# A pooling and state-space layer on one core: decode states turned together, and staged through DRAM

## The chip, the cores and the metric

The kernel runs on one core of a Trainium2 chip. TensorE multiplies matrices (PE in the profile; PEld is its loading of weights), VectorE is DVE, ScalarE is ACT, GpSimd is POOL, and SyncE (SP) issues DMAs. ACT issues DMAs too. Sixteen DMA engines move the data. The metric is the time of one execution on the device in microseconds, as the median of several runs.

## The reference

One layer is applied to a prompt (1 x 1024 tokens) and to eight decode samples of 8 tokens each. The model width is 1024; the input projection has 8224 columns.

```python
h = rmsnorm(x, norm_g) * (1 + scale[:, None]) + shift[:, None]
u_pool, z_pool, z_ssm, xbc, dt_raw, g_raw = jnp.split(h @ w_in, SPLITS, axis=-1)
p, pool_new = pool_mix(u_pool, pool_buf, pos0, pool_w, pool_scale)   # last 15 input rows kept
p = (p * jax.nn.silu(z_pool)) @ w_pool_out
xbc_c, conv_new = causal_conv(xbc, conv_buf, conv_w, conv_b)         # width 4, last 3 rows kept
y, ssm_new = ssd(xs, dt, A, Bm, Cm, ssm_state)                       # 32 heads of 64 x 128
y = rmsnorm((y + d_skip * xs) * jax.nn.silu(z_ssm), ssm_norm_g)
m = gates[..., :D_MODEL] * p + gates[..., D_MODEL:] * (y @ w_ssm_out)
x = x + gate[:, None] * (m @ w_o)
```

The samples bring states from earlier steps: `state_pool` (8 x 15 x 512), `state_conv` (8 x 3 x 3072) and `state_ssm` (8 x 32 x 64 x 128). The prompt starts from zero. The outputs are y for prompt and samples and the new states of both: the last 15 pooling rows, the last 3 convolution rows and the state matrices. Everything is float32.

## The kernel before

Channels lie on the 128 partitions and tokens along the free axis, 1088 of them: 1024 of the prompt, then 64 of the samples. A product in float32 is made of three passes in fp32r, a faster format, on operands that are split into a high and a low part; the split takes ACT (`whi`) and POOL or DVE (`wlo`).

The program has four stages. The first (`first`) normalizes x, makes the adaLN factors and starts the projection. The second goes through `units`, pairs of 128 columns of `w_in`. Each pair is one Strassen product of seven half products (`product`, lines 609 to 611), and its two column blocks go to a generator that finishes them: `to_dram` for the gates ("light" pairs), `conv_unit`, `u_unit` and `zp_unit` ("heavy" pairs). The steps of a generator that come after its product wait in the list `later` and are taken out one by one between the half products of the next pair (`between`, `step`); what is left is taken at the last. Beside the pairs runs `splits`, which prepares weights of later stages and sends them to DRAM.

The third stage runs the last ten light pairs with `samples_beside`: first the steps of `dt_end`, then for each of four head groups `ssd_samples`, 18 steps apiece, spread evenly. The fourth does the prompt's chunks, the output products and the norms; its loop is not touched.

The order of instructions on an engine in the first stage and the last is written out by hand (`in_line`). In the second and third stage a planner orders them by a simulated time line; `behind(engine)` only says that an instruction comes after the last one on an engine that was written before it. Each queue of DMA issues runs in order, so a DMA that waits holds those behind it. A tile with `bufs=n` has n slots in rotation; a new tile waits until the slot's last user is done.

What the change touches:

- `conv_unit` (line 1031): per block of 128 channels it loads the samples' 24 state rows into `stc`, turns them on PE (1039) and lets ACT copy them (1040). Later it collects the last rows of prompt and samples in `t27` (1049, 1051), turns them (1067), copies them (1069), and ACT issues two stores (1070, 1071). This happens for 24 blocks.
- `u_unit` (757): the same for four blocks with 120 state rows (`stp`, 760, 775, 776), and with turns of the 15 and 64 last rows (805, 806).
- `ssd_samples` (1223): `h0_load` (1239) reads four batches of two heads straight from `state_ssm` into one of four tiles `h0`, in runs of 512 bytes. A step turns four 128 x 128 blocks with a float32 identity (1304), copies them (1306), and `update` (1288) makes the new state in place in `h0` (1294), which ACT's queue stores (1296).
- `turn_r` (117): a turn in fp32r, so far used by the chunk stage alone; its instructions have line 118.
- `dt_end` (1077): loads the raw dt rows into `s0`, a tile of tag `dec`, and turns them (1109).
- `to_conv` (1553): closes the first stage's right-hand memory and opens that of the convolutions, whose big tiles have tag `GA` (seven slots).

Of the kernel before, what the change touches and what calls it, by code (L numbers as in the profile page):

```python
# [8 lines left out]
F32 = mybir.dt.float32  # L9
# [37 lines left out]
def tile_pool_ssd_step(  # L47
# [9 lines left out]
    def nm(s):  # L57
        uid[0] += 1
        return f"{s}_{uid[0]}"
# [36 lines left out]
    def PB():  # L96
        return psB.tile([P, 512], F32, tag="ps", name=nm("ps"))
# [40 lines left out]
    nc.gpsimd.memset(rc[:, 0:1], 1.0)  # L138
    vb = sm.tile([44, P], F32, tag="stc", name="vb", bufs=4)
    store_(vb[0:16, :], b_ada[0, 0:2048].rearrange("(m p) -> m p", p=P))  # L140
# [231 lines left out]
    def late_loads():  # L372
        va = sm.tile([120, P], F32, tag="stc", name="va", bufs=4)
# [7 lines left out]
        dx = sm.tile([16, 2, 64], F32, tag="stc", name="dx", bufs=4)  # L381
# [375 lines left out]
    def u_unit(gi):  # L757
        L = gi + 1
        stp = sm.tile([120, P], F32, tag="stc", name=nm("stp"), bufs=4)
        load(stp, state_pool[0, :, :, gi * P:(gi + 1) * P].rearrange("b t c -> (b t) c"))  # L760
        pwt = sm.tile([P, P], F32, tag="stc", name=nm("pwt"), bufs=4)
        load(pwt, pool_w[0, gi])
# [10 lines left out]
        V.memset(up[:, 0:15], 0.0)  # L773
        ps = PB()
        nc.tensor.transpose(ps[:, :120], stp, ident[:120, :120])
# [34 lines left out]
        store_(new_pool_p[0, 0, :, gi * P:(gi + 1) * P], o15)  # L810
        store_(new_pool_s[0, :, 7:15, gi * P:(gi + 1) * P], o64)
        y = up[:, :T]
# [216 lines left out]


    def conv_unit(mc, dst):
# [7 lines left out]
        nc.tensor.transpose(ps[:, :24], stc, ident[:24, :24])  # L1039
        act(seg[:, :, 0:3], ps[:, :24].rearrange("p (b t) -> p b t", t=3), AF.Copy)  # L1040

# [23 lines left out]
        store_(dst[:, SEQ:], s64.rearrange("p b t -> p (b t)"))  # L1065
        ps = PB()
        nc.tensor.transpose(ps[:27, :P], t27, ident)
# [9 lines left out]
    def dt_end():  # L1077
# [145 lines left out]
    def ssd_samples(g):  # L1223
# [5 lines left out]
        load_E(E2, g)  # L1229
        dec = spt([P, 8, P], "dec", 2)[:NS, :, :NS]  # L1230
        decays(dec, g, NC)
# [4 lines left out]
        def h0_load(j):  # L1236
            hf, q = divmod(j, 4)
            h0 = spt([P, 4, P], "h0", H0B)
            load(h0, state_ssm[0, 4 * hf:4 * hf + 4, 8 * g + 2 * q:8 * g + 2 * q + 2].rearrange("b h p n -> (h p) b n"))
            h0s[j] = h0  # L1240
# [19 lines left out]
        for hf in range(2):  # L1260
# [27 lines left out]
            def update(r):  # L1288
                h0 = h0s.pop(4 * hf + r)
                pu = PB()  # L1290
                mm(pu, xh[:96, r * P:(r + 1) * P], Bb[:96].rearrange("p b n -> p (b n)"), start=True, stop=True)
                for b in range(4):
                    cc_ = 32 * hf + 8 * b + 7
                    V.scalar_tensor_tensor(h0[:, b, :], h0[:, b, :], E2[:, r, cc_:cc_ + 1],
                                           pu[:, b * P:(b + 1) * P], ALU.mult, ALU.add)
                store_(new_ssm_s[0, 4 * hf:4 * hf + 4, 8 * g + 2 * r:8 * g + 2 * r + 2]
                       .rearrange("b h p n -> (h p) b n"), h0)
            for q in range(4):
# [4 lines left out]
                for b in range(4):  # L1303
                    nc.tensor.transpose(pt[:, b * P:(b + 1) * P], h0s[j][:, b, :], ident)
                hts[q] = spt([P, 512], ("hT", "yt", "hU", "hV")[q], 1)
# [247 lines left out]
    def to_conv():  # L1553
        nonlocal right
        right.__exit__(None, None, None)
        right = tc.tile_pool(name="ga", bufs=1, side="right", reuse_waits="tile")
        gas.append(right.__enter__())

    def to_ssd():
# [291 lines left out]
    def m_split(k, mem):  # L1851

        sh = sm.tile([P, P], F32R, tag="stc", name=nm("sh"), bufs=4)
        act(sh[:, 0:NS], acc[k][:, SEQ:], AF.Copy)
# [200 lines left out]
```

## Time and profile before

| | us |
|---|---|
| median of 3 runs | 1273.08 (1272.99 to 1273.53) |
| the profiled execution | 1271.29 |
| its span, first to last instruction | 1269.5 |
| PE busy | 1242.3 (98%) |
| DVE busy | 900.9 (71%) |
| ACT busy | 718.0 (57%) |
| POOL busy | 683.1 (54%) |

The profile page has the busy time of each engine, the costliest groups of instructions, and the DMA queues. Queries to the trace give the busy time by stretch, the waits (an engine and line that waited, who ended it, total us, number and longest), all instructions of one line (minimum, median and longest duration in ns, first and last start), and a timeline. Matmuls are pipelined: the next starts before the last has ended, so durations on PE overlap and start times tell more. Sixteen engines share the DMA packets; they carried 234.90 MB in this execution.

### The profile page before, as it was taken

What the parts mean: (1) busy time and instruction counts of PE and PEld (TensorE: products, weight loads), DVE (VectorE), ACT (ScalarE), POOL (GpSimd) and SP (SyncE); (2) the same over time, 40 slices, a digit from 0 to 9 for tenths busy, and PEclk for the clock granted to TensorE, in tenths of its full rate; (3) what the DMA queues carried; (4) which work ended last, traced back from release to release, by engine and by line L of the source; (5) the groups of instructions that cost most, each with busy time, mean ns of one, the idle gap of its engine ahead of it and who ended that gap; (6) DMA issues with size and microseconds to landing.
All of it is one profiled execution on the core that took longest, in us unless ns stands there. A gap on an engine that the chain in (4) does not pass through costs nothing. (4 is left out here: it accounts for less than half of the span.)

```text
span 1269.5 us, 26341 instructions
## 1 busy us (share of the span) xinstructions
PE 1242.3 (98%) x9771; PEld 1173.9 (92%) x9771; DVE 900.9 (71%) x1584; ACT 718.0 (57%) x1683; POOL 683.1 (54%) x555
## 2 busy tenths in 40 slices
PE   7999999999999999999999999999999999999997
PEld 6779999999999999998989999999999999999786
DVE  4695678966979588975756665598677879766543
ACT  4665356474666656554554554687887768522211
POOL 1007669886878777764344454365565646545000
PEclk9999999999999999999999999999999999999999
DMA  9937354565456454443557445899766567485431
GB/s 332 298 104 226 116 167 161 181 204 160 138 182 201 146 182 164 149 138 116 157 142 226 151 147 167 283 300 319 217 200 201 181 212 206 152 291 179 149 108 50
DMA packets 225729, 234.90 MB, mean 185 GB/s; under 512 B 30369, under 2 KB 177009, under 8 KB 225594
## 3 DMA queue, kind: packets, MB, share of 16 engines
q1 hardware_dynamic: 155808, 159.01, 40.3%
q10 hardware_dynamic: 69794, 74.22, 17.4%
q8 instruction: 77, 1.26, 0.4%
q14 instruction: 50, 0.41, 0.1%
HBM read 158.67 MB, written 74.62 MB: 184 GB/s over the span
## 5 line engine op out<-in xcount | busy, mean ns | idle before, releaser
L169 POOL TENSOR_TENSOR wlo<-rawA,whi 128x512 fp32r<-128x512 f32 x120 | 189.0, 1580 | 170.5 <-ACT whi L166 95.8
L169 POOL TENSOR_TENSOR wlo<-raw,whi 128x512 fp32r<-128x512 f32 x92 | 155.1, 1693 | 122.2 <-ACT whi L166 119.3
L360 PE MATMUL mm<-Y,whi 128*128 128x352 f32 (+1 forms) x480 | 159.8, 333 | 0.7
L361 PE MATMUL mm<-Y,whi 128*128 128x352 f32 (+1 forms) x480 | 157.3, 328 | 0.4 <-DVE Y L1516 0.4
L362 PE MATMUL mm<-Y,wlo 128*128 128x352 f32 (+1 forms) x480 | 156.8, 327 | 0.0
L609 PE MATMUL mm<-Y,whi 128*128 128x272 f32 x496 | 146.3, 295 | 2.2 <-ACT whi L166 2.2
L611 PE MATMUL mm<-Y,wlo 128*128 128x272 f32 x496 | 143.5, 290 | 2.5 <-POOL wlo L169 2.0
L609 PE MATMUL ps<-Y,whi 128*128 128x272 f32 x496 | 143.8, 290 | 0.0
L610 PE MATMUL ps<-Y,whi 128*128 128x272 f32 x496 | 143.0, 288 | 0.0
L610 PE MATMUL mm<-Y,whi 128*128 128x272 f32 x496 | 142.9, 288 | 0.0
L611 PE MATMUL ps<-Y,wlo 128*128 128x272 f32 x496 | 142.5, 287 | 0.0
L1057 DVE SCALAR_TENSOR_TENSOR GA<-GA,cvT,GA 128x1112 f32<-128x1112 f32 x72 | 126.6, 1763 | 0.1
L166 ACT ACTIVATE whi<-rawA 128x512 fp32r<-128x512 f32 x125 | 78.1, 627 | 81.1 <-PE ps L610 44.0
L166 ACT ACTIVATE whi<-raw 128x512 fp32r<-128x512 f32 x96 | 58.9, 627 | 97.6 <-DVE raw L555 51.7
L609 PEld LDWEIGHTS mm<-Y,whi 128*128 128x128 f32 x496 | 93.5, 189 | 4.2 <-ACT whi L166 2.8
L611 PEld LDWEIGHTS mm<-Y,wlo 128*128 128x128 f32 x496 | 93.5, 189 | 2.9 <-POOL wlo L169 2.2
L360 PEld LDWEIGHTS mm<-Y,whi 128*128 128x128 f32 x480 | 90.3, 188 | 4.2 <-DVE G L1890 2.4
L610 PEld LDWEIGHTS mm<-Y,whi 128*128 128x128 f32 x496 | 93.5, 189 | 0.7 <-issue 0.6
L610 PEld LDWEIGHTS ps<-Y,whi 128*128 128x128 f32 x496 | 93.3, 188 | 0.4
L609 PEld LDWEIGHTS ps<-Y,whi 128*128 128x128 f32 x496 | 93.3, 188 | 0.2
L611 PEld LDWEIGHTS ps<-Y,wlo 128*128 128x128 f32 x496 | 93.4, 188 | 0.0
L361 PEld LDWEIGHTS mm<-Y,whi 128*128 128x128 f32 x480 | 90.3, 188 | 2.6 <-DVE Y L1516 0.9
(464 smaller groups left out, 3821.9 us busy)
## 6 DMA issues: line engine op xcount, KB each, us to landing
rawA<-in_w_in SPq DMA_DIRECT2D x46, 512.0 KB
dec<-acs_d SPq DMA_DIRECT2D x32, 512.0 KB
xbc<-GA ACTq DMA_DIRECT2D x24, 512.0 KB
xb<-xbc SPq DMA_DIRECT2D x32, 384.0 KB
rawA<-in_w_in SPq DMA_DIRECT2D x32, 256.0 KB
pw<-in_w_ssm_out ACTq DMA_DIRECT2D x32, 256.0 KB
ws<-ph ACTq DMA_DIRECT2D x32, 256.0 KB
ws<-pw SPq DMA_DIRECT2D x32, 256.0 KB
```

What stands on the lines that cost most here:

```text
L166: ins = act(hi[:, :, :ncols], raw[:, :, :ncols], AF.Copy)
L169: (eng or nc.gpsimd).tensor_tensor(lo[:, :, :ncols], raw[:, :, :ncols], hi[:, :, :ncols].bitcast(F32), ALU.subtract)
L360: mm(ps[:, :n], a, rh[k][:, o:o + n], start=(k == 0), stop=False)
L361: mm(ps[:, :n], a, rl[k][:, o:o + n], start=False, stop=False)
L362: mm(ps[:, :n], b, rh[k][:, o:o + n], start=False, stop=(k == nk - 1))
L609: mm(p, hi, ah, start=(k == 0), stop=False)
L610: mm(p, hi, al, start=False, stop=False)
L611: mm(p, lo, ah, start=False, stop=(k == 3))
L1057: V.scalar_tensor_tensor(d[:, :n], rp[:, k:k + n], cvT[:, 24 * k + mc:24 * k + mc + 1], d[:, :n], ALU.mult, ALU.add)
```

## The change

The states of convolution and pooling are loaded once, right after the first stage, into two `GA` tiles (576 and 480 rows of 128 numbers, in blocks of 128 rows), and `turn_states` turns them in nine turns into two tiles that stay. `conv_unit` and `u_unit` copy their part from there with a stride.

The last rows of convolution are collected for six blocks at a time (four of x, and B and C of a head group) in one tile of 162 columns. When the sixth block is done, two turns and two copies follow, and twelve stores that SP issues instead of ACT. In the pooling units the 15 and 64 last rows stand in one tile of 79 columns and are turned once.

The samples' `state_ssm` is moved by 32 DMAs from DRAM to DRAM, into scratch laid out as `h0` needs it; one is issued each four steps of the second stage, from SP. `h0_load` reads the scratch. The turns of `h0` use `turn_r`. The update writes to a tile of its own, `hn`, with two slots. The samples' `dec` tile has half the size, and `s0` in `dt_end` takes a slot of `rawA`, the weights' ring. The tag `stc` has three slots instead of four.

```diff
     def u_unit(gi):
         L = gi + 1
-        stp = sm.tile([120, P], F32, tag="stc", name=nm("stp"), bufs=4)
-        load(stp, state_pool[0, :, :, gi * P:(gi + 1) * P].rearrange("b t c -> (b t) c"))
-        pwt = sm.tile([P, P], F32, tag="stc", name=nm("pwt"), bufs=4)
+        pwt = sm.tile([P, P], F32, tag="stc", name=nm("pwt"), bufs=3)
...
         V.memset(up[:, 0:15], 0.0)
-        ps = PB()
-        nc.tensor.transpose(ps[:, :120], stp, ident[:120, :120])
-        V.tensor_copy(us[:, :, 0:15], ps[:, :120].rearrange("p (b t) -> p b t", t=15))
-        u64 = sm.tile([P, NB, 8], F32, tag="rsm", name=nm("u64"))
-        act(u64, us[:, :, 15:23], AF.Copy)
-        u15 = sm.tile([P, 27], F32, tag="t27", name=nm("u15"))
-        act(u15[:, 0:15], up[:, SEQ:SEQ + 15], AF.Copy)
-        yield
+        V.tensor_copy(us[:, :, 0:15], pool_t[0].rearrange("p (b t m) -> p b t m", t=15, m=4)[:, :, :, gi])
+        yield
+        u79 = sm.tile([P, 79], F32, tag="u79", name=nm("u79"), bufs=1)
+        act(u79[:, 15:].rearrange("p (b t) -> p b t", t=8), us[:, :, 15:23], AF.Copy)
+        act(u79[:, 0:15], up[:, SEQ:SEQ + 15], AF.Copy)
...
-        nc.tensor.transpose(ps[:15, :P], u15[:, 0:15], ident)
-        nc.tensor.transpose(ps[:NS, P:2 * P], u64.rearrange("p b t -> p (b t)"), ident)
-        o15, o64 = [sm.tile([n, P], F32, tag="o27", name=nm("o15")) for n in (15, NS)]
-        act(o15, ps[:15, :P], AF.Copy)
-        act(o64, ps[:NS, P:2 * P], AF.Copy)
+        nc.tensor.transpose(ps[:79, :P], u79, ident)
+        o79 = sm.tile([79, P], F32, tag="o79", name=nm("o79"), bufs=1)
+        act(o79, ps[:79, :P], AF.Copy)
...
     def conv_unit(mc, dst):
-        stc = sm.tile([24, P], F32, tag="stc", name=nm("stc"), bufs=4)
-        load(stc, state_conv[0, :, :, mc * P:(mc + 1) * P].rearrange("b t c -> (b t) c"))
         yield
...
-        ps = PB()
-        nc.tensor.transpose(ps[:, :24], stc, ident[:24, :24])
-        act(seg[:, :, 0:3], ps[:, :24].rearrange("p (b t) -> p b t", t=3), AF.Copy)
+        act(seg[:, :, 0:3], conv_t[0].rearrange("p (b t m) -> p b t m", t=3, m=24)[:, :, :, mc], AF.Copy)
...
-        t27 = sm.tile([P, 27], F32, tag="t27", name=nm("t27"))
+        g, i = (mc // 4, mc % 4) if mc < 16 else (mc % 4, mc // 4)
+        if not i:
+            t27s[g] = sm.tile([P, 6 * 27], F32, tag="t27", name=nm("t27"))
+        t27 = t27s[g][:, 27 * i:27 * i + 27]
...
-        ps = PB()
-        nc.tensor.transpose(ps[:27, :P], t27, ident)
-        o27 = sm.tile([27, P], F32, tag="o27", name=nm("o27"))
-        act(o27, ps[:27, :P], AF.Copy)
-        store_(new_conv_p[0, 0, :, mc * P:(mc + 1) * P], o27[0:3])
-        store_(new_conv_s[0, :, :, mc * P:(mc + 1) * P], o27[3:27])
+        if i == 5:
+            ps = PB()
+            o27 = sm.tile([108, 2 * P], F32, tag="o27", name=nm("o27"))
+            for c, n in ((0, 108), (1, 54)):
+                nc.tensor.transpose(ps[:n, c * P:c * P + P], t27s[g][:, 108 * c:108 * c + n], ident)
+                act(o27[:n, c * P:c * P + P], ps[:n, c * P:c * P + P], AF.Copy)
+            for j, m in enumerate((4 * g, 4 * g + 1, 4 * g + 2, 4 * g + 3, 16 + g, 20 + g)):
+                r, c = j % 4 * 27, j // 4 * P
+                with behind(mybir.EngineType.SP):
+                    load(new_conv_p[0, 0, :, m * P:(m + 1) * P], o27[r:r + 3, c:c + P])
+                    load(new_conv_s[0].rearrange("b t c -> (b t) c")[:, m * P:(m + 1) * P], o27[r + 3:r + 27, c:c + P])
+                yield
...
-        s0 = sp.tile([P, 8 * P], F32, tag="dec", name="s0", bufs=2)
+        s0 = pa.tile([P, 8 * P], F32, tag="rawA", name="s0", bufs=5)
...
-        dec = spt([P, 8, P], "dec", 2)[:NS, :, :NS]
+        dec = spt([P, 8, NS], "dec", 2)[:NS]
...
-            load(h0, state_ssm[0, 4 * hf:4 * hf + 4, 8 * g + 2 * q:8 * g + 2 * q + 2].rearrange("b h p n -> (h p) b n"))
+            load(h0, h0_d[8 * g + j])
...
             def update(r):
                 h0 = h0s.pop(4 * hf + r)
                 pu = PB()
+                hn = spt([P, 4, P], "hn", 2)
...
-                    V.scalar_tensor_tensor(h0[:, b, :], h0[:, b, :], E2[:, r, cc_:cc_ + 1],
+                    V.scalar_tensor_tensor(hn[:, b, :], h0[:, b, :], E2[:, r, cc_:cc_ + 1],
...
-                       .rearrange("b h p n -> (h p) b n"), h0)
+                       .rearrange("b h p n -> (h p) b n"), hn)
...
-                    nc.tensor.transpose(pt[:, b * P:(b + 1) * P], h0s[j][:, b, :], ident)
+                    turn_r(pt[:, b * P:(b + 1) * P], h0s[j][:, b, :])
...
+        for src, rows in ((state_conv, 576), (state_pool, 480)):
+            flat = src[0].rearrange("b t (m p) -> (b t m) p", p=P)
+            st, full = GA([P, 5, P]), rows // P
+            with behind(mybir.EngineType.SP):
+                load(st[:, :full], flat[:full * P].rearrange("(a r) p -> r a p", r=P))
+            with behind(mybir.EngineType.SP):
+                load(st[:rows - full * P, full], flat[full * P:])
+            states.append((st, rows))
+
+    def turn_states():
+        for (st, rows), kept_in in zip(states, (conv_t, pool_t)):
+            out = small([P, rows], "st%d" % rows, 1)
+            for a in range(0, rows, 512):
+                ps = PB()
+                e = min(rows, a + 512)
+                for r in range(a, e, P):
+                    n = min(P, e - r)
+                    nc.tensor.transpose(ps[:, r - a:r - a + n], st[:n, r // P], ident[:n, :n])
+                act(out[:, a:e], ps[:, :e - a], AF.Copy)
+            kept_in.append(out)
...
-    units = [plain(to_conv), light[1], plain(pool_rows)]
+    units = [plain(to_conv), light[1], plain(turn_states), plain(pool_rows)]
...
+    h0_d = [dram(f"h0{n}", [P, 4, P]) for n in range(32)]
+
+    def move_states():
+        for n in range(32):
+            g, hf, q = n // 8, n // 4 % 2, n % 4
+            with behind(mybir.EngineType.SP):
+                load(h0_d[n], state_ssm[0, 4 * hf:4 * hf + 4, 8 * g + 2 * q:8 * g + 2 * q + 2].rearrange("b h p n -> (h p) b n"))
+            for _ in range(4):
+                yield
+    moved = move_states()
...
-    run_units(units, 1, lambda: next(pre, None))
+    run_units(units, 1, lambda: (next(pre, None), next(moved, None)))
```

More of the change, by code (lines that the diff above doesn't have):

```diff
@@ L138, in tile_pool_ssd_step @@
     nc.gpsimd.memset(rc[:, 0:1], 1.0)
-    vb = sm.tile([44, P], F32, tag="stc", name="vb", bufs=4)
+    vb = sm.tile([44, P], F32, tag="stc", name="vb", bufs=3)
     store_(vb[0:16, :], b_ada[0, 0:2048].rearrange("(m p) -> m p", p=P))
@@ L372, in late_loads @@
     def late_loads():
-        va = sm.tile([120, P], F32, tag="stc", name="va", bufs=4)
+        va = sm.tile([120, P], F32, tag="stc", name="va", bufs=3)
         load(va[0:96, :], conv_w[0].rearrange("k (m p) -> (k m) p", p=P))
@@ L380, in late_loads @@
         yield
-        dx = sm.tile([16, 2, 64], F32, tag="stc", name="dx", bufs=4)
+        dx = sm.tile([16, 2, 64], F32, tag="stc", name="dx", bufs=3)
         V.tensor_copy(dx, dk.unsqueeze(2).to_broadcast([16, 2, 64]))
@@ L804, in u_unit @@
         ps = PB()
-        nc.tensor.transpose(ps[:15, :P], u15[:, 0:15], ident)
-        nc.tensor.transpose(ps[:NS, P:2 * P], u64.rearrange("p b t -> p (b t)"), ident)
-        o15, o64 = [sm.tile([n, P], F32, tag="o27", name=nm("o15")) for n in (15, NS)]
-        act(o15, ps[:15, :P], AF.Copy)
-        act(o64, ps[:NS, P:2 * P], AF.Copy)
-        store_(new_pool_p[0, 0, :, gi * P:(gi + 1) * P], o15)
-        store_(new_pool_s[0, :, 7:15, gi * P:(gi + 1) * P], o64)
+        nc.tensor.transpose(ps[:79, :P], u79, ident)
+        o79 = sm.tile([79, P], F32, tag="o79", name=nm("o79"), bufs=1)
+        act(o79, ps[:79, :P], AF.Copy)
+        store_(new_pool_p[0, 0, :, gi * P:(gi + 1) * P], o79[0:15])
+        store_(new_pool_s[0, :, 7:15, gi * P:(gi + 1) * P], o79[15:79])
         y = up[:, :T]
@@ L1026, in first @@
         in_line(every)
+    t27s = {}
     def conv_unit(mc, dst):
-        stc = sm.tile([24, P], F32, tag="stc", name=nm("stc"), bufs=4)
-        load(stc, state_conv[0, :, :, mc * P:(mc + 1) * P].rearrange("b t c -> (b t) c"))
         yield
@@ L1557, in to_conv @@
         gas.append(right.__enter__())
+        for src, rows in ((state_conv, 576), (state_pool, 480)):
[17 more added lines that the diff above has]
+            kept_in.append(out)
+    states, conv_t, pool_t = [], [], []
     def to_ssd():
@@ L1851, in m_split @@
     def m_split(k, mem):
-        sh = sm.tile([P, P], F32R, tag="stc", name=nm("sh"), bufs=4)
+        sh = sm.tile([P, P], F32R, tag="stc", name=nm("sh"), bufs=3)
         act(sh[:, 0:NS], acc[k][:, SEQ:], AF.Copy)
```

## The prediction

> **What bounds the kernel now.** I read the page first, then stretches of the span by engine, then who waited for whom on PE, then single stretches of PE's timeline. Stretches: length, then busy time (and instructions) of PE, PEld, DVE, ACT, POOL, then granted clock, DMA share, GB/s.
>
> ```profile
> span 1269.5 us, 26341 instructions
> PE 1242.3 (98%) x9771; PEld 1173.9 (92%) x9771; DVE 900.9 (71%) x1584; ACT 718.0 (57%) x1683; POOL 683.1 (54%) x555
> ```
>
> ```profile
> 0.00:70.00 70.00, 58.71 (x525) 49.38 (x525) 42.24 (x110) 40.53 (x73) 5.11 (x33) 1.00 0.93 304
> 140.00:556.00 416.00, 416.00 (x3280) 410.17 (x3279) 331.92 (x498) 239.31 (x572) 322.97 (x199) 1.00 0.51 166
> 556.00:830.00 274.00, 266.35 (x2299) 255.40 (x2297) 174.84 (x407) 151.61 (x329) 122.58 (x95) 0.99 0.58 175
> ```
>
> ```profile
> PE mm L609 <- ACT whi L166: 2.2, 3, 1.1
> PE mm L611 <- POOL wlo L169: 2.0, 1, 2.0
> PE mm L609 <- DVE u L620: 1.2, 1, 1.2
> PE ps L1291 <- DVE dec L1275: 1.0, 2, 0.6
> ```
>
> PE is the bound. In the convolution and pooling stage (140 to 556) it is busy for all of 416.00 us; in the stage of the samples and of the last light pairs (556 to 830) for 266.35 of 274. The four waits shown (total us, times, longest) fall mostly in that second stage; they sum to 6.4 us. So an instruction taken off PE there shortens the run by what it costs PE, as long as no new wait comes; one taken off ACT, DVE or SP shortens nothing.
>
> "Busy" doesn't give that cost, since matmuls overlap. I take it from start times: how much later the matmuls behind an inserted turn start. (Columns: start, length, engine and line, output and inputs, count.)
>
> ```profile
> 169.74 0.29 PE L609 MATMUL mm<-Y,whi 128*128 128x272 f32 x1
> 169.87 0.29 PE L610 MATMUL mm<-Y,whi 128*128 128x272 f32 x1
> 169.99 0.29 PE L611 MATMUL mm<-Y,wlo 128*128 128x272 f32 x1
> 170.21 0.30 PE L1039 MATMUL ps<-ident,stc 24*128 24x24 f32 x2
> 170.44 0.39 PE L609 MATMUL mm<-Y,whi 128*128 128x272 f32 x1
> 170.66 0.29 PE L610 MATMUL mm<-Y,whi 128*128 128x272 f32 x1
> ...
> 177.67 0.27 PE L1067 MATMUL ps<-ident,t 128*27 128x128 f32 x1
> 177.70 0.37 PE L609 MATMUL mm<-R,whi 128*128 128x272 f32 x1
> 177.91 0.29 PE L610 MATMUL mm<-R,whi 128*128 128x272 f32 x1
> ...
> 551.80 1.14 PE L1109 MATMUL ps<-ident,s 128*128 128x128 f32 x9
> 552.91 0.29 PE L610 MATMUL ps<-R,whi 128*128 128x272 f32 x1
> ...
> 628.04 0.60 PE L1304 MATMUL ps<-ident,h 128*128 128x128 f32 x4
> 628.61 0.29 PE L610 MATMUL mm<-G,whi 128*128 128x272 f32 x1
> ...
> 853.75 0.55 PE L118 MATMUL ps<-identR,xb 128*128 128x128 f32 x5
> 854.13 0.46 PE L1415 MATMUL ps<-xb 128*128 128x128 f32 x2
> ```
>
> Product matmuls start 0.125 us apart (169.74, 169.87, 169.99). Behind 169.99 the next L609 and L610 were due at 170.12 and 170.24; with two state turns between, L610 is at 170.66: 0.42 us for two. By the same count one turn of last rows (L1067) costs 177.91 - 177.67 - 0.125 = 0.11; nine full turns in a run 552.91 - 551.80 - 0.125 = 0.98, so 0.11 each; four turns of a sample's state (L1304) 628.61 - 628.04 - 0.125 = 0.44, again 0.11 each. Five of fp32r (L118) take 0.38 to the next instruction: 0.076 each.
>
> **The change part by part.** How often each stands in the program:
>
> ```profile
> L1039 PE MATMUL ps<-ident,stc x24: 213/226/238, 144.8 to 496.8; 24*128 24x24 f32 x24
> L1067 PE MATMUL ps<-ident,t x24: 271/271/272, 177.7 to 539.4; 128*27 128x128 f32 x24
> L775 PE MATMUL ps<-ident,stp x4: 266/267/268, 144.6 to 451.3; 120*128 120x120 f32 x4
> L1304 PE MATMUL ps<-ident,h x128: 270/272/303, 607.3 to 782.6; 128*128 128x128 f32 x128
> L118 PE MATMUL ps<-identR,xb x160: 222/249/254, 810.0 to 1089.0; 128*128 128x128 f32 x160
> ```
>
> *States in one run.* 24 conv turns go: 12 x 0.42 = 5.0 us of PE. Four pool turns (L775) go, at 0.11: 0.4. Nine turns of the joined states come (576 and 480 rows): 1.0. Two of the nine are short blocks (64 and 96 rows); if a short block costs as the 24-row ones do, 0.21, it is 0.2 more; all nine at 0.21 is the end, 1.9. Net -4.4, between -3.5 and -4.4.
>
> *Last rows by groups.* 24 turns (L1067) at 0.11 go, 2.6 us; eight come (four groups of two), 0.9. The pool's eight turns (L805, L806, four each) become four of 79 columns: -0.4. Net -2.2.
>
> So the conv stage gives -6.6 us. What goes with it from ACT (24 copies of 27 rows become eight, 48 issues of stores go to SP) and from SP (28 small loads) was hidden under a PE that never idled, so it is costed at nothing; the copy of a conv state out of SBUF instead of PSUM likewise, ACT being busy 239 of 416 us.
>
> *Turns in fp32r.* 128 x (0.110 - 0.076) = -4.4 us. The trace has no fp32r turn in this stage, so bounds: 0, if the spacing of L118 is that of its neighbours; -4.4 by the spacing, which I take since it is measured on the same shape. By durations (272 against 249 ns) it would be -2.9, but a turn's duration isn't what it costs PE: four in 0.44 us.
>
> [...]
>
> *The tile for the update (hn).* DVE now writes the new state into one of two tiles, so the third update of a run waits until the first store has landed. Before, the update was in place and the load of a later state, on SP, waited:
>
> ```profile
> SPq L1239 <- DMA out<-h: 103.5, 28, 18.9
> SPq L541 <- POOL wlo L169: 187.9, 37, 15.6
> ```
>
> ```profile
> 630.07 2.15 DVE L1294 SCALAR_TENSOR_TENSOR h<-h,hst,ps 128x128 f32<-128x128 f32 x8
> 631.22 1.41 ACTq L1296 DMA_DIRECT2D out<-h  x2
> 634.17 1.12 DVE L1294 SCALAR_TENSOR_TENSOR h<-h,hst,ps 128x128 f32<-128x128 f32 x4 [0.24 <-PE ps L1291]
> 635.57 1.05 SPq L1239 DMA_DIRECT2D h<-in_state_ssm  x2
> ```
>
> Here the stores of updates one and two are issued from 631.22, the third update starts at 634.17, and SP's load, which waits for the first store, goes out at 635.57. So the third update would have waited up to 635.57 - 634.17 = 1.4 us. Queued behind it on DVE are the combinations of the Strassen products (L620, L625), which free PE's PSUM buffers. DVE is busy 174.84 of 274 us there and PE has waited for it (L620) once, 1.2 us, so I charge 0.5 us; the ends are 0 and 16 such waits (third and fourth update of eight runs) uncovered, 22 us. [...]
>
> *States through DRAM.* The nearest row is the load that these transfers feed, same size and count:
>
> ```profile
> L1239 SPq DMA_DIRECT2D h<-in_state_ssm x32: 367/368/1115, 589.2 to 772.2; - x32
> ...
> h<-in_state_ssm SPq DMA_DIRECT2D x32, 256.0 KB
> ```
>
> 32 transfers of 256 KB go from DRAM to DRAM during the conv stage, 8.4 MB in 416 us: 20 GB/s more, or 40 with the writes counted apart. At the present 0.51 for 166 GB/s this is 0.06 to 0.12 of DMA share, so 0.57 to 0.63, under the 0.93 of the first stretch. SP issues them without a wait, 32 x 0.37 us, and 48 stores of last rows more, which wait for ACT's copy. Behind them stand the weights' loads (L541). Those already wait up to 15.6 us for their tile with PE full, so the cover is large: nothing. If it were gone, a move ahead of a load delays it by 256 KB at 166 GB/s, 1.6 us. In the sample stage the 32 loads keep their size; they become rows of 2 KB, cost taken as nothing.
>
> ```profile
> L522 DVE TENSOR_TENSOR tf<-tf,tf x4: 714/714/719, 85.6 to 91.7; 128x544 f32<-128x544 f32 x4
> 84.20 1.34 SPq L857 DMA_DIRECT2D gate_d<-bg  x4
> 96.37 0.95 SPq L544 DMA_DIRECT2D rawA<-in_w_in  x2
> ```
>
> *The states' own loads* wait for tiles of the first stage; the last that lie there are read by L522 at 91.7. SP has nothing between 85.5 and 96.37, so four loads fit without holding the weights of 96.37. The turns come behind the first light pair, later still. The dt tile in the weights' ring (rawA) holds one of five slots for some steps; the pairs need four. Nothing for either.
>
> **Sum.** -6.6 - 4.4 + 0.5 = -10.5 us. The profiled execution took 1271.3 us (span 1269.5 and 1.8 around it), 1.8 under the median of 1273.1. It becomes 1260.8; the median, moved by the same, 1262.6.
>
> **The rivals.**
>
> *The store's wait takes it back (slower).* Place: DVE's third and fourth update of each run, behind hn. 16 waits of 1.4 us, uncovered, are 22.4 us: 1273.1 - 11.0 + 22.4 = 1284.5. It ends the gain at 11.0/16 = 0.7 us each, and is slower by a measurable 2.5 us from 0.85 us each. For it: 103.5 us of SP's waits are for these stores. Against it: DVE idles 99 us of this stage, and most runs of updates are spread over several products.
>
> *The turns in fp32r are no cheaper.* Both kinds last nearly the same (272 and 249 ns); then only -6.6 + 0.5 stays: 1267. The 0.076 us, in 160 turns, speak against it. [...]
>
> *The moves and stores on SP delay weights.* Break-even at 11/32 = 0.34 us of PE for each move: 1273 to 1275. Against it: SP's slack above. The change would then show no difference.
>
> *The order of the sample stage comes out better.* The instructions there are ordered anew by the planner's simulation; the four waits (6.4 us) could mostly vanish: about 1257. They could as well grow by as much: 1269, still faster.
>
> **How the numbers follow.** A measurement of this kernel can tell about 0.2%, 2.5 us. Chances: the sum within 1259 to 1266, 0.56; fp32r no cheaper, or the new order a few us worse (1266 to 1270.5), 0.16; better order (under 1259), 0.08; moves in the way (1270.5 to 1275.6), 0.07; stores' wait (over 1275.6), 0.13. So faster 0.80, same 0.07, slower 0.13. The time is the sum's, 1262.6. The range, 1257 to 1273, leaves out the slow case, half of the moves and a little below.
>
> **What would show it.** PE should have some 39 turns fewer (each one record) and the matmul count otherwise unchanged; the state turns in one run of nine before 144.6 us, where the first L775 stood; the stretch from the first light pair to the last conv unit shorter by 6 to 7 us with PE still full; turns of h0 listed under L118 at 0.076 us spacing. Wrong would be: waits of DVE's update for a DMA of hn that PE then shares, PE waiting for whi or wlo in the conv stage, or h0's turns still 0.11 us apart.

## The result: no difference

Measured side by side on one chip, 14 runs each: before 1275.01 us at the median, after 1274.85 us. The ratio is 1.0004, 95% interval 0.9991 to 1.0018. Forecast were 1262.6 us and a gain, so the prediction was wrong by its whole gain.

The profiled execution of the changed kernel took 1270.02 us, the fastest of its 14 (they reach to 1279.23). Its span is only 1.2 us under that of before, so it shows some of the loss and not all of it. The page's head and its first part:

```profile
span 1268.3 us, 26199 instructions
PE 1236.7 (98%) x9732; PEld 1169.5 (92%) x9732; DVE 910.1 (72%) x1584; ACT 717.8 (57%) x1668; POOL 680.4 (54%) x555
```

PE has 39 instructions fewer (9771 before) and is busy 5.6 us less, but its share of the span stays at 98%: part of what it no longer does, it waits. Where, these stretches show: the convolution stage as in the prediction, then the sample stage and the opening of the chunk stage, each cut at the starts of the same products (given below), and one short stretch (columns as in the prediction: length, busy time of PE, PEld, DVE, ACT, POOL, granted clock, DMA share, GB/s), first after:

```profile
140.00:556.00 416.00, 415.87 (x3285) 412.62 (x3284) 343.62 (x510) 240.46 (x556) 322.38 (x199) 1.00 0.57 182
556.77:806.61 249.84, 241.94 (x2119) 231.60 (x2117) 157.57 (x376) 130.83 (x278) 115.44 (x89) 0.99 0.54 163
806.61:840.63 34.02, 30.50 (x232) 27.75 (x232) 27.48 (x43) 28.82 (x80) 12.02 (x12) 1.00 0.84 278
640.00:655.00 15.00, 12.85 (x101) 12.10 (x100) 7.07 (x16) 11.72 (x24) 7.55 (x6) 0.89 0.30 93
```

and of before, the same two stages and a short stretch, which the prediction did not show:

```profile
561.53:810.60 249.07, 243.20 (x2119) 233.67 (x2117) 154.12 (x377) 129.45 (x275) 116.59 (x89) 0.99 0.56 167
810.60:842.44 31.84, 30.06 (x232) 27.79 (x232) 27.47 (x43) 28.24 (x77) 12.00 (x12) 1.00 0.80 262
600.00:610.00 10.00, 7.92 (x62) 7.09 (x60) 4.41 (x9) 6.75 (x18) 3.06 (x3) 0.83 0.37 107
```

The convolution stage is as forecast: PE full (415.87 of 416), DMA share 0.57, up from 0.51. In the sample stage PE is busy for 1.3 us less than before and idle for 2.0 us more (7.9 us of 249.84, where it was 5.9 of 249.07). In the opening of the chunk stage it is idle for 1.7 us more. Both kernels have one place where PE ran at a lower granted clock: before around 604, after around 646.

The lengths of the stages come from the starts of the same product in both timelines: the first of the second of the ten last light pairs, when the convolution blocks are done, the first of the chunk stage's products (L360), and the 121st L360 to L362 product. Before:

```profile
561.53 0.29 PE L609 MATMUL mm<-Y,whi 128*128 128x272 f32 x1
...
810.60 0.42 PE L360 MATMUL mm<-Y,whi 128*128 128x384 f32 x1
...
842.44 0.32 PE L360 MATMUL mm<-Y,whi 128*128 128x352 f32 x1
```

After:

```profile
556.77 0.28 PE L609 MATMUL mm<-Y,whi 128*128 128x272 f32 x1
...
806.61 0.42 PE L360 MATMUL mm<-Y,whi 128*128 128x384 f32 x1
...
840.63 0.33 PE L360 MATMUL mm<-Y,whi 128*128 128x352 f32 x1
```

| stretch, us | before | after | difference | forecast |
|---|---|---|---|---|
| to the end of the convolution stage | 561.53 | 556.77 | -4.8 | -6.6 |
| sample stage | 249.07 | 249.84 | +0.8 | -3.9 |
| opening of the chunk stage | 31.84 | 34.02 | +2.2 | 0 |
| the rest | 427.1 | 427.7 | +0.6 | 0 |

The first gain is real. The second did not come, and the third row was in no term of the sum. PE's waits after (total us, times, longest):

```profile
PE mm L609 <- ACT whi L166: 5.9, 6, 2.1
...
PE ps L118 <- DVE btl L1445: 2.1, 1, 2.1
...
PE ps L1214 <- DVE dec L1440: 1.1, 1, 1.1
```

PE waited for whi, ACT's part of the weights, 2.2 us in all before and 5.9 now, while its waits for wlo and u in the sample stage fell from 3.2 to 1.4 us; the other two waits lie in the opening of the chunk stage. DVE's update waits five times for a store of hn:

```profile
DVE hn L1295 <- DMA out<-hn: 7.9, 5, 2.4
```

Three things stand behind all this, and the experiments take them apart: two slots for hn, a split group of Exp on ACT, and a load that waits for a tile's place.

The split group stands in ACT's timeline of the changed kernel (643.15 is the whi that PE waited for):

```profile
639.86 1.28 ACT L721 ACT_TABLE_LOAD   x1
641.15 0.43 ACT L721 ACTIVATE s<-s 128x272 f32<-128x272 f32 x1
641.60 1.28 ACT L1202 ACT_TABLE_LOAD   x1
642.89 0.35 ACT L1202 ACTIVATE dec<-dec,acT 64x64 f32<-64x64 f32 x1
...
643.15 1.14 ACT L166 ACTIVATE whi<-raw 128x512 fp32r<-128x512 f32 x2
```

and in the timeline of all engines of the same stretch:

```profile
638.05 1.78 ACT L1202 ACTIVATE dec<-dec,acT 64x64 f32<-64x64 f32 x7 [0.79 <-POOL dec L1197]
...
643.82 0.39 PE L609 MATMUL mm<-Y,whi 128*128 128x272 f32 x1 [2.15 <-ACT whi L166]
```

Seven of the eight Exp of a head group, a table load of 1.28 us, one function of another table, a second load, the eighth Exp, and only then whi. The planner had set one piece of a light pair between the seventh and the eighth Exp. Before, no table load stands among the eight of any group.

### The profile page after: what moved, and what is told of

Same layout as the page of the kernel before. It is cut to its first block, busy times and chain, and to the rows that moved or that the text cites. A ratio compares the mean times of both kernels' runs of the same rounds, so it can differ in the third digit from the quotient of the medians.

```text
span 1268.3 us, 26199 instructions
## 1 busy us (share of the span) xinstructions
PE 1236.7 (98%) x9732; PEld 1169.5 (92%) x9732; DVE 910.1 (72%) x1584; ACT 717.8 (57%) x1668; POOL 680.4 (54%) x555
## 5 line engine op out<-in xcount | busy, mean ns | idle before, releaser
L169 POOL TENSOR_TENSOR wlo<-rawA,whi 128x512 fp32r<-128x512 f32 x120 | 192.3, 1609 | 153.7 <-ACT whi L166 82.4
L169 POOL TENSOR_TENSOR wlo<-raw,whi 128x512 fp32r<-128x512 f32 x92 | 147.3, 1608 | 136.5 <-ACT whi L166 122.0
L360 PE MATMUL mm<-Y,whi 128*128 128x352 f32 (+1 forms) x480 | 160.2, 334 | 0.9 <-DVE G L1922 0.4
L362 PE MATMUL mm<-Y,wlo 128*128 128x352 f32 (+1 forms) x480 | 157.0, 327 | 0.0
L360 PEld LDWEIGHTS mm<-Y,whi 128*128 128x128 f32 x480 | 90.2, 188 | 4.6 <-DVE G L1922 2.6
```

Source lines behind the costliest of these rows:

```text
L169: (eng or nc.gpsimd).tensor_tensor(lo[:, :, :ncols], raw[:, :, :ncols], hi[:, :, :ncols].bitcast(F32), ALU.subtract)
L360: mm(ps[:, :n], a, rh[k][:, o:o + n], start=(k == 0), stop=False)
L362: mm(ps[:, :n], b, rh[k][:, o:o + n], start=False, stop=(k == nk - 1))
```

## The experiments

Times are medians. The kernel before ran beside each group of kernels (1273.8 us for the first four, 1274.2 for the next four, 1274.8 for the last three), so kernels of different groups are compared by their ratios to it: 0.001 is 1.27 us. Differences are worked out so where nothing else is said.

**The convolution stage alone.** The changed kernel with everything of the samples' states undone (the update is in place again, and the tiles `dec` and `s0` are as before):

```diff
-            load(h0, h0_d[8 * g + j])
+            load(h0, state_ssm[0, 4 * hf:4 * hf + 4, 8 * g + 2 * q:8 * g + 2 * q + 2].rearrange("b h p n -> (h p) b n"))
...
-                hn = spt([P, 4, P], "hn", 2)
...
-                    turn_r(pt[:, b * P:(b + 1) * P], h0s[j][:, b, :])
+                    nc.tensor.transpose(pt[:, b * P:(b + 1) * P], h0s[j][:, b, :], ident)
...
-    run_units(units, 1, lambda: (next(pre, None), next(moved, None)))
+    run_units(units, 1, lambda: next(pre, None))
```

> The changed kernel with its conv and pooling parts alone; the samples' states are read, turned (float32) and updated in place as before. My account of the two traces says the conv stage gains about 5.5 us and that what is lost lies behind it. Theory A (the sample stage loses by the order that the planner now writes there, above all ACT's Exp group split by a Sigmoid, with a further table load): the conv stage is 5 to 6 us shorter, the sample stage no longer than before give or take 2, so 1268 to 1270 against 1274 (ratio 0.995 to 0.997). Theory B (the lost gain is the wait for hn's store): the same here, as there is no hn. Theory C (the gain of the conv stage is given back later whatever comes behind, since the chunk stage starts when its loads have landed): ratio 0.998 to 1.0, the chunk stage's start no earlier than 2 us before that of the kernel before.

1269.66 us, ratio 0.9966 (0.9948 to 0.9983). This half of the change is a gain of about 4.3 us, which the chunk stage does not take back: theory C is out.

**The samples' states alone**, the other half, put into the kernel before.

> The kernel before with the sample-state parts alone: moves through DRAM scratch, fp32r turns, the tile hn, the smaller dec tile, s0 in the weights' ring. The turns give back 128 x 0.018 = 2.3 us of PE by the spacing in the changed kernel's trace. Theory A: the split Exp group is there too, so the sample stage is 1 to 5 us longer: ratio 1.000 to 1.004. Theory B: DVE waits for hn's store for about 8 us and the stage is longer by the part of it that PE shares, up to 5 us: the same ratio, but with PE's waits behind DVE. Theory C: no change, 0.999 to 1.001.

1278.52 us, ratio 1.0033 (1.0013 to 1.0052). This half is a loss of about 4.2 us, and the two cancel. The question is then why this half loses, when its turns cost PE less.

**A third slot for hn.**

```diff
-                hn = spt([P, 4, P], "hn", 2)
+                hn = spt([P, 4, P], "hn", 3)
```

> The changed kernel with three tiles hn instead of two; ACT's order of Exp and Sigmoid is the same as in the changed kernel. Theory B: DVE's 7.9 us of waits for the store go to under 1 and the sample stage shortens by 3 to 5 us, ratio to the kernel before 0.996 to 0.997. Theory A: the waits go, but the stage keeps its long waits for ACT (about 2 us near 644): at most 1.5 us gained, ratio 0.999.

1265.83 us, ratio 0.9933 (0.9907 to 0.9958): 9 us faster than the changed kernel, more than either theory gave it. DVE no longer waits for a store of hn, but the split Exp group and PE's stall behind it (2.87 us here) are still there. And the opening of the chunk stage is 2.4 us shorter too, which slots don't explain at once.

**The Exp group ahead in the planner's order.** Two slots; the eight Exp of a head group get priority, and stand together.

```diff
-        exps(dec, g, NC)
+        with tc.high_priority(PRIO):
+            exps(dec, g, NC)
```

> The changed kernel with one edit: the eight Exp of a sample's decay get a high priority, so that the planner writes them in one run on ACT. Theory A: one pair of table loads (2.6 us of ACT) goes, PE's wait of 2.3 us for whi near 644 goes and with it the 3.4 us at half clock behind it: the sample stage shorter by 3 to 5 us, ratio to the kernel before 0.996 to 0.998. Theory B: nothing, ratio 1.000, hn's waits stay at 8 us. If other waits come up in its place, the planner's order as such is the cause and not the split.

1270.33 us, ratio 0.9968 (0.9951 to 0.9986): 4.6 us faster than the changed kernel. The stall at 644 is gone, but one of 2.7 us came at 693. So theory A holds in part, and B too: neither is the whole.

**Two slots in the room of three**, the last third of each tile unused.

```diff
-                hn = spt([P, 4, P], "hn", 2)
+                hn = spt([P, 6, P], "hn", 2)[:, 0:4]
```

> The changed kernel with each hn tile half again as large (6 by 128 instead of 4 by 128 columns, the last third unused): the room of three tiles, but two slots. Theory L (place in memory): the opening of the chunk stage lost 2.2 us in the changed kernel because its first load had to wait for the samples' last store, whose tile lies where the load goes; moved by 2 KB the two no longer meet. Then the wait of SP for ys (25.1 us) is gone, the opening (first to 120th matmul group of the chunk stage) is 2.2 to 2.5 us shorter than in the changed kernel, and the sample stage stays as it was there, DVE's waits for hn among them (7.9 us): 2.4 us faster than the changed kernel in all, 1271.5 to 1273 at the median. Theory S (slots): all 4.5 us that the third slot brought came from DVE not waiting, the opening's too, by timing; then this kernel equals the changed one, 1274 to 1276, with SP's wait for ys still there.

1272.01 us, ratio 0.998 (0.9967 to 0.9993), 3 us faster than the changed kernel, with intervals that just meet. The instructions of all engines stand in the same order as in the changed kernel; only the place of tiles differs. Theory L came out. SP's waits and its timeline, first in the changed kernel:

```profile
SPq L1388 <- DMA ys<-xd: 25.1, 1, 25.1
```

```profile
791.06 0.56 SPq L1388 DMA_DIRECT2D xb<-xbc  x1
```

and with the wider tiles:

```profile
SPq L1388 <- DMA gs<-c: 14.1, 1, 14.1
```

```profile
784.35 0.56 SPq L1388 DMA_DIRECT2D xb<-xbc  x1
```

The stage's first product starts at 806.61 in the one and 811.01 in the other, so the first load of xb runs 15.5 us ahead of it in the changed kernel and 26.7 us with the wider tiles (before 23.3, by the row below). In the changed kernel it waits for the samples' last store to ys to land. The two have no data in common. What they can have in common is the place: `to_chunks` closes the samples' memory and opens that of xb in its stead, the halved dec and the new hn moved the tiles, and with 2 KB more the wait is gone. (The traces don't show the addresses.) The other kernels bear it out: in the five with two slots of the normal size (the changed kernel, the samples' states alone, the Exp group ahead, and two with float32 turns that follow below) SP waits 23.7 to 25.5 us for ys and the opening takes 33.7 to 36.3 us; in the six that give hn the room of three slots that wait does not occur and the opening takes 31.5 to 32.0 us. The same load before:

```profile
787.28 0.55 SPq L1387 DMA_DIRECT2D xb<-xbc  x1
```

The opening runs at a DMA share of 0.84 and doesn't catch up: 34.02 us, against 31.84 before and 32.03 with the wider tiles, from these two starts:

```profile
811.01 0.42 PE L360 MATMUL mm<-Y,whi 128*128 128x384 f32 x1
...
843.04 0.33 PE L360 MATMUL mm<-Y,whi 128*128 128x352 f32 x1
```

DVE's waits for hn (8.1 us) and PE's stall near 644 (2.48 us) stayed. The sample stage is 3.4 us longer in this profile than in that of the changed kernel, the fastest of its runs; the order is the same, and an estimated 1.7 us of it lie in a second stretch at half clock behind that stall (3.41 us at 0.50; the granted clock from 640 to 655 is 0.77, where the changed kernel has 0.89).

**Both: three slots, and the Exp group together.**

```diff
-        exps(dec, g, NC)
+        with tc.high_priority(PRIO):
+            exps(dec, g, NC)
...
-                hn = spt([P, 4, P], "hn", 2)
+                hn = spt([P, 4, P], "hn", 3)
```

> The changed kernel with three slots for hn and the sample's Exp group put ahead in the planner's order, so that its eight Exp stand together between two loads of ACT's table. Theory A (a split Exp group holds up ACT's halves of the operand, and PE with it): the waits of PE for ACT's whi in the sample stage (5.9 us) go, and the half-clock stretch behind them, so 2 to 3 us less than with three slots alone: 1262.5 to 1264 beside 1265.8. Theory P (each new order of the planner's has stalls of its own of some 2 us at one place or another): within 1.5 us of three slots alone on either side, 1264.5 to 1267.5, with one or two PE stalls over 1.5 us at other places.

1262.23 us, ratio 0.9921 (0.9894 to 0.9947), the fastest kernel of the study: 10 us faster than before by the ratio (12 by the medians), which is the size of the gain that the prediction had forecast for the change as it stood, though by two edits that it did not have. PE's waits:

```profile
PE mm L609 <- ACT whi L166: 2.6, 4, 1.2
```

and its stretches (the sample stage, and the one that had held the stall):

```profile
556.96:801.17 244.21, 239.66 (x2119) 229.88 (x2117) 159.85 (x377) 128.63 (x277) 116.17 (x89) 1.00 0.57 171
640.00:655.00 15.00, 13.52 (x116) 12.59 (x115) 9.99 (x21) 9.99 (x23) 9.62 (x7) 1.00 0.40 119
```

The sample stage takes 244.21 us, 4.9 less than before (forecast: 3.9 less), with the clock full throughout. Theory A came out in the profile: the stall and the half clock behind it are gone, and the stage is 3.9 us shorter than with three slots alone (248.06). The runs show it less clearly: 3.6 us by the medians and 1.5 by the ratios, whose intervals overlap.

**The same with two slots of half again the size** (places as with three, the Exp group together):

```diff
-                hn = spt([P, 4, P], "hn", 3)
+                hn = spt([P, 6, P], "hn", 2)[:, 0:4]
```

> The best kernel so far (three hn slots, the Exp group together) with two slots of half again the size instead of three: same room, same place of all other tiles, nearly the same order. Theory S (the third slot saves DVE's waits and these reach PE): the sample stage is 1.5 us or more longer than with three slots (244.2 us there), DVE waits some 5 to 8 us for its stores, a PE stall of 2 us or more comes back and with it the half clock: 1264.5 to 1268. Rival O (only the order matters, DVE's waits are covered): 1261.5 to 1263.5, with the same 0.999 clock.

1269.06 us, ratio 0.9957 (0.9941 to 0.9974): 4.6 us slower than with three slots by the ratios, 6.8 by the medians; the intervals just overlap. Theory S came out in kind: the median is above its range (1264.5 to 1268), and the PE stall that came back (1.91 us, to 695.68) has no half clock behind it in the profile: products from 697.46 to 698.73 start 0.127 us apart. The sample stage takes 249.0 us by the profile, 4.8 more. DVE waits for its stores:

```profile
DVE hn L1296 <- DMA out<-hn: 8.0, 5, 2.5
```

But these waits aren't all of it. The planner, which knows the slots, sets a slightly other order. ACT with two slots:

```profile
691.79 1.28 ACT L1202 ACT_TABLE_LOAD   x1
693.09 2.02 ACT L1202 ACTIVATE dec<-dec,acT 64x64 f32<-64x64 f32 x8
695.02 0.61 ACT L166 ACTIVATE whi<-raw 128x512 fp32r<-128x512 f32 x1
```

and with three:

```profile
689.97 0.63 ACT L166 ACTIVATE whi<-raw 128x512 fp32r<-128x512 f32 x1 [1.00 <-DVE raw L555]
690.62 1.28 ACT L1202 ACT_TABLE_LOAD   x1
691.91 2.02 ACT L1202 ACTIVATE dec<-dec,acT 64x64 f32<-64x64 f32 x8
```

With two, whi stands behind the table load and eight Exp, and PE waits for it:

```profile
695.68 0.40 PE L609 MATMUL mm<-Y,whi 128*128 128x272 f32 x1 [1.91 <-ACT whi L166]
```

How much of the difference is DVE's waiting and how much the order can't be told from these runs: the order changes with the slots.

**float32 turns, in the changed kernel and in the best one.**

```diff
-                    turn_r(pt[:, b * P:(b + 1) * P], h0s[j][:, b, :])
+                    nc.tensor.transpose(pt[:, b * P:(b + 1) * P], h0s[j][:, b, :], ident)
```

> The changed kernel with the 128 turns of the samples' states in float32 again; the move through DRAM and the hn tile stay. By the spacing measured in the changed kernel, four fp32r turns hold up PE for 0.368 us and four float32 turns for 0.440: 32 times 0.072 is 2.3 us, so the sample stage is 2.3 us longer than in the changed kernel, at equal waits: 1277. Rival (the turns' form is worth nothing, because PE waits for other engines in this stage whatever it saves): within 0.7 us of the changed kernel. Second rival (the prediction's figure, 4.4 us): 1279.

> The best kernel so far with the turns of the samples' states in float32. There no PE stall is over 1.4 us, so the turns should show at their price: 32 groups of four at 0.440 instead of 0.368 us, 2.3 us more, 1264.5. Rival 1 (worth nothing: the stage is held by the other engines): within 0.7 us, 1261.5 to 1263. Rival 2 (the prediction's 0.110 against 0.076 us each): 4.4 us more, 1266.6.

In the changed kernel 1273.06 us, ratio 0.9991 (0.9978 to 1.0005): no loss at all, the time of the first rival. Its reason is not shown, since the planner's order changed with the turns: DVE waits 3.8 us for hn instead of 7.9, and the pair that starts at 669.1 in the changed kernel takes 26.8 us instead of 28.7, about what the turns cost more. In the best kernel 1264.54 us, ratio 0.9937 (0.9914 to 0.9959): 2.0 us more by the ratios and 2.3 by the medians. That is what the spacing gives, but the intervals overlap widely, and here too the order changed. So the price of the turns rests on the spacing. In the changed kernel:

```profile
724.72 0.29 PE L611 MATMUL ps<-G,wlo 128*128 128x272 f32 x1
724.85 0.46 PE L118 MATMUL ps<-identR,h 128*128 128x128 f32 x4
725.14 0.36 PE L611 MATMUL mm<-Y,wlo 128*128 128x272 f32 x1
725.34 0.28 PE L609 MATMUL mm<-Y,whi 128*128 128x272 f32 x1
```

and with float32 turns in the best one:

```profile
721.28 0.29 PE L611 MATMUL ps<-G,wlo 128*128 128x272 f32 x1
721.41 0.60 PE L1306 MATMUL ps<-ident,h 128*128 128x128 f32 x4
721.76 0.37 PE L611 MATMUL mm<-Y,wlo 128*128 128x272 f32 x1
721.97 0.28 PE L609 MATMUL mm<-Y,whi 128*128 128x272 f32 x1
```

From the product ahead of the four turns to the second behind them, less two steps of 0.125: 725.34 - 724.72 - 0.25 = 0.37 us in fp32r, 721.97 - 721.28 - 0.25 = 0.44 us in float32. The first step behind the turns is 0.20 us, not 0.125, in both. Of the 32 groups of a kernel twelve or thirteen stand free between products; they cost 0.36 to 0.38 us in the changed kernel, and 0.44 to 0.45 us before and with float32 turns in the best one.

**The loads straight from the input**, in the same two kernels (float32 turns, no move through DRAM):

```diff
-            load(h0, h0_d[8 * g + j])
+            load(h0, state_ssm[0, 4 * hf:4 * hf + 4, 8 * g + 2 * q:8 * g + 2 * q + 2].rearrange("b h p n -> (h p) b n"))
...
-    run_units(units, 1, lambda: (next(pre, None), next(moved, None)))
+    run_units(units, 1, lambda: next(pre, None))
```

> The changed kernel with float32 turns and without the move of the states through DRAM: the samples' loads come from the input as before, the hn tile stays. Beside the float32 run above it this prices the move alone. Prediction's reasoning (the moves are hidden under a full PE): the conv stage is the same within 0.5 us, the sample stage the same within 1 us. Rival M (the 32 moves and their issue on SP hold up the weights): the conv stage is 1 to 3 us shorter without them. Rival R (loads of 2 KB rows from the scratch are quicker than those of 512-byte pieces from the input): the sample stage is 1 to 3 us longer here, with more waits of PE for h0.

> The one before it, float32 turns too, with the samples' loads straight from the input and no move through DRAM. Prediction's reasoning: nothing, within 0.7 us of it. From the earlier pair of such runs (conv stage 0.6 us shorter without the moves, sample stage equal) I expect 0.3 to 0.8 us less: 1263.7 to 1264.2 where that one has 1264.5. Rival R (2 KB rows quicker): 1 us or more longer.

1271.99 us (0.9987, 0.9973 to 1.0002) beside 1273.06 with the move, and 1265.48 us (0.9943, 0.9921 to 0.9965) beside 1264.54. The signs differ and the intervals overlap: no difference that can be told, as the prediction had it. On the computing engines the order is the same within each pair, save for two instructions of DVE. In both pairs of profiles the convolution stage, counted from the second pair on (103 us), was 0.6 us shorter without the moves.

## Why the prediction was wrong, step by step

*States in one run, last rows by groups* (-6.6). Mechanism right, size nearly: the convolution stage took 4.8 us less by the profile, and the part alone is worth 4.3 us in the runs. Of the missing 1.8 us, 0.2 is the run of nine turns, which cost 1.2 us instead of 1.0, as the prediction's own variant for short blocks had it, from the product ahead of it and the first behind it:

```profile
124.14 0.29 PE L611 MATMUL ps<-Y,wlo 128*128 128x272 f32 x1
124.26 1.36 PE L1576 MATMUL ps<-ident,GA 128*128 128x128 f32 x9
125.41 0.37 PE L609 MATMUL mm<-Y,whi 128*128 128x272 f32 x1
```

(125.41 - 124.14 - 0.125 = 1.15, and the first step behind is longer). Some 0.6 was lost ahead of that, in the first stage, where kernels with the same start vary by up to 2.3 us. The moves account for 0.6 to 0.7, by which the stage is shorter without them; the last 0.3 stays open.

*Turns in fp32r* (-4.4). Mis-sized: 32 x (0.44 - 0.37) = 2.3 us by the spacing, and the best kernel with and without them differs by 2.0 to 2.3, within the noise of those runs. The step read 0.076 us as the cost of a turn from a row of five and the start behind it; it left out that the product behind a run of turns takes 0.20 us to the next instead of 0.125. It had counted the float32 turns to 0.44, that delay included. The rival that they are no cheaper is out by the spacing; the runs alone can't rule it out, and in the changed kernel float32 turns, with the order that came with them, were as good (0.9991 against 1.0004).

*The tile for the update, two slots* (+0.5). **This is the step that failed.** With the turns it was to make the samples' states a gain of 3.9 us; alone they are a loss of 4.2. A third slot is worth 4.6 us with the Exp group together, and 6.0 in the changed kernel (0.998 against 0.9933, equal places). The rival "the store's wait takes it back" named this wait, at about four times the size. What was wrong was the reason for 0.5: DVE's share of 175 in 274 us, an average over the stage. The waits are few and long (five, up to 2.4 us), DVE's combinations stand behind them, and the planner, knowing the slots, sets another order, whi behind the Exp in it. A tile of their own need not be bad for the updates: with three slots, loads from the input and float32 turns as before, and the Exp group together, the ratio is 0.9943, where the update in place without the Exp together has 0.9966; the intervals overlap. No run has two slots beside the update in place with all else equal, so the true price of the +0.5 is not shown.

*What was in no step*, and so put at nothing. First, the place of tiles: halving dec and adding hn were costed by what they do, not by what they lie on. By the kernel with wider tiles that gave SP's 25.1 us wait and 2.2 us in the opening of the chunk stage. Second, the new order as such: the prediction let it go either way by about 6 us, and it did both. The stall of before near 602 went (the 33.2 us from the pair that starts at 584.37 to the next are 28.8 after), and the split Exp group came, worth 4.6 us by the run that put it together with two slots, and 1.5 to 3.6 with three. Third, the clock. In the profiles of before and after the half-clock stretch in the sample stage follows one of these PE stalls, and the mean granted clock of the runs differs too: 0.9939 over the 14 runs after, 0.9964 over 29 of before (those beside the experiments), 0.9972 in the best kernel. A difference of 0.0025 is 3.2 us of a span of 1270. With the span times (1 - clock) taken off the time of each run, the runs of before are 1269.6 us on average and those after 1267.2: without the clock the change would show an estimated 2.4 us.

*Hidden work.* DMA share 0.57 is the lower end of the forecast, PE did not wait for weights in the convolution stage, and the moves cost 0.6 us or so of it, which the whole time doesn't show. The states' loads and s0 in the weights' ring were priced by no run of their own.

Put together: convolution stage -4.3 and samples' states +4.2. In the second, turns -2.3 by the spacing, two slots instead of three +4.6 to +6.0, place of tiles +2 to +3, split Exp +1.5 to +4.6; on the other side the stall of before that went, and what a tile of its own for the update brings. Each was taken in another surrounding, with an order of its own, so they don't add up; their signs, and their sizes to some 2 us, are what the runs show.

## What to carry to other kernels

Where a planner orders the work, a change has two prices: that of its own instructions, which spacing in the trace gives to a few tenths, and that of the order it brings, which can be as large and is seen only in the new profile. So look there first for engine stalls over 1 us and what stands ahead of them on the releasing engine; here putting eight Exp together and giving a tile one more slot brought the 10 us that the change alone had not. A smaller tile isn't free either: it moves its neighbours, and here a load then waited for a store that it has nothing to do with, so read what each first load of a stage waits for.

## Hardware behaviour that was not expected

The clock. The profiles have stretches of 3.41 us, once or twice in a row, in which PE was granted half its clock (0.50). In the changed kernel one begins at 645.9, 2.1 us after the 2.15 us stall ended, and the row for 640 to 655 above has 0.89. In the best kernel, without a stall over 1.4 us in that stage, the same stretch has 1.00. In the changed kernel's stretch products start 0.227 us apart (647.10 to 648.46), and 0.126 behind it (649.35 to 649.98). Where PE is the bound, such a stretch costs on top of the stall an estimated 1.5 us by this spacing, 3.41 x (1 - 0.126/0.227), or 1.7 by the granted clock, half its length.

Before, a stall of 2.00 us had such a stretch behind it; in the changed kernel one of 2.15 us had, and one of 2.06 us had none. Within each profile the stretches begin whole multiples of 3.4133 us apart, to 0.01 us: before at 603.93 and 1266.11, 194 multiples apart, after at 645.91 and 1267.13, 182 (the last of each lies at the end of the span); in the changed kernel with float32 turns at 623.36, 647.26, 824.75 and 1114.88, which is 7, 59 and 144 multiples behind the first. So in these profiles the starts lie on one grid, and the span can be cut into windows by it. Two windows of before, then two of after:

```profile
600.52:603.93 3.41, 1.41 (x12) 1.19 (x11) 0.00 (x0) 2.00 (x8) 2.54 (x3) 1.00 0.45 133
603.93:607.34 3.41, 3.41 (x29) 3.00 (x28) 1.91 (x5) 2.70 (x6) 0.00 (x0) 0.50 0.52 154
```

```profile
819.98:823.39 3.41, 2.00 (x15) 1.83 (x13) 2.06 (x2) 3.38 (x10) 0.63 (x1) 1.00 0.97 305
823.39:826.80 3.41, 2.77 (x21) 2.58 (x23) 3.41 (x8) 3.39 (x11) 1.50 (x2) 1.00 0.94 291
```

The 2.0 us stall of before lies in one window, and the next has half the clock. The stall of 2.06 us in the changed kernel is split by a boundary into 1.42 and 0.64 us, and the clock stays full; that of 2.15 us is split too, into 0.82 and 1.33 us, and the window behind has half the clock. In the thirteen profiles, between 90 and 1255 us, PE idled for 1.9 us or more in ten windows at full clock, and all ten had half the clock behind them; of twelve windows with 1.3 to 1.9 us three had it, of 4381 with less two. In these two windows PE counts as busy, but for 2.05 us it did 18 products of one column each; in the other eleven kernels a boundary splits the same 18 products, and none has half the clock behind them. So in these profiles the half clock goes with the time within one window in which PE does little: ten times of ten with 1.9 us idle or more, three of twelve with 1.3 to 1.9. What sets the clock is not shown. No run moved one stall alone, so this is read from the traces and not tested.

An fp32r turn of 128 columns costs PE 0.092 us in a group of four (0.37), a float32 one 0.11. The saving is a sixth; the durations of the two (246 and 272 ns) would make it a tenth.
